# Program order for four engines in an expert loop, and a row finished in the front

## The chip, the cores and the metric

The kernel runs on one core of a Trainium2 chip. The metric is the device time of one execution in microseconds (us); lower is better. The engines are PE (TensorE, matrix products), DVE (VectorE), ACT (ScalarE), POOL (GpSimd) and SP (SyncE); each works off its own queue of instructions in order. Transfers run on 16 DMA engines, whichever engine issued them. Granted clock 1.00 means that TensorE runs at 2.4 GHz, 0.50 that it runs at 1.2 GHz.

## What is computed

One decoder layer on 512 tokens of width 1024, in float32. A mixer (a state-space branch and a block-sparse attention branch) is followed by a mixture of 32 experts, of which each token uses four. The part of the reference that matters here, cut:

```python
ada = cond @ ada_w[l] + ada_b[l]
sh_m, sc_m, gt_m, sh_f, sc_f, gt_f = split(ada, 6)
...
h2 = rms_norm(x, ffn_pre_g[l]) * (1.0 + sc_f) + sh_f
# moe_ffn(h2): every token goes to its top four experts
g = xb @ w_gate[e] + b_gate[e]
u = xb @ w_up[e] + b_up[e]
g = min(g, LIMIT); u = clip(u, -LIMIT, LIMIT)
yb = (g * sigmoid(ALPHA * g) * (u + 1.0)) @ w_down[e] + b_down[e]
y[row_tok] += yb * row_w
...
x = x + gt_f * rms_norm(ff, ffn_post_g[l])
```

The weights of one expert are three matrices of 1024 x 1024 floats (4 MB each), so the expert loop moves 384 MB of weights. `gt_f` is the last of the six gates that come from `ada_w`.

## The kernel before

**The front** (up to about 550 us) computes the mixer, the gates and the routing. `row_part` (lines 692 to 715) makes one half of one gate row: `cond_times` accumulates `ada_w` on DVE, a matmul with ones sums over the partitions. For the last gate (`name` is None) the row goes to `gfd` in memory as it is, a copy on ACT and a store on ACT's queue.

**The expert loop** (lines 1444 to 1458) walks over `jobs`. There are 32 slots, one expert each, sorted by how many tokens they hold; a slot has one or two blocks of 128, 64 or 32 tokens. A job is one of gate, up and down of a slot, in the order gate(n+1), down(n), up(n+1). `project` (line 1243) works a job off in four pieces of 1 MB of weights. Slots with a block of 128 split the weights into high halves (ACT, line 111) and low halves (DVE, line 112), one piece ahead of use, and multiply with three matmuls (lines 116 to 118). The other blocks multiply float32 weights as they are (line 1269).

**The weights** come through a ring of 11 chunks of 1 MB (`RINGS`), loaded by SP's queue (lines 1118 to 1122). A chunk is loaded again when the matmuls, or the splits, that read it are done.

**The small work of a slot.** `prep` (line 1164) makes a one-hot table `oh` on DVE and calls `tokens` (line 1194). `tokens` looks up the slot's rows with PE (line 1184), computes `src` and `dst` on DVE (lines 1205 and 1213) and issues the gather of the tokens into `xg` on POOL (line 1207). `weights` looks up the routing weights. `load` transposes `xg` on PE (line 1227 for blocks of up to 64, line 1237 for 128) through two PSUM buffers `tr`, and ACT or ACT and DVE copy the result out. Behind a job comes its stage function: `gate` (Silu on ACT), `up` (two DVE instructions into `s`, then the transposition of `s` into `a`), `down` (scaling on ACT into `yo`, then a scatter that adds into `yd`, issued by POOL at line 1313). `dst` has six buffers, `src` three, `oh` two.

**What sets the order.** `prep` and `weights` of slot n+1 are written ahead of the gate job of slot n, and `load` of slot n+1 is appended to `later` behind down(n-1). The rest goes through a list `later`: `follow(1)` behind each piece runs one entry of it. But these places only give priorities. A scheduler places each instruction on its engine, and may move it ahead of others or behind them by what it expects to be ready. POOL's order is set by hand only for a stretch before the loop (`manual_schedule` with POOL).

**The last row.** Behind the loop, `out_g` is loaded from `gfd` for all partitions, and two rows of 128 x 1024 (512 KB each, `ada_b` and `ffn_post_g`) are loaded by ACT's queue (line 1455) into `row`, which shares its buffers with the tokens of 128-token blocks, and are added to it and multiplied in on DVE (line 1456). The scheduler puts these into the loop where it finds room. The tail (from line 1473) normalizes the sum of the experts and writes the output.

Of the kernel before, what the change touches and what calls it, by code (L numbers as in the profile page):

```python
# [8 lines left out]
F32 = mybir.dt.float32  # L9
# [5 lines left out]
ALU = mybir.AluOpType  # L15
AX = mybir.AxisListType

P = 128
# [53 lines left out]
def tile_hybrid_block(ctx: ExitStack, tc: tile.TileContext, A, out):  # L72
# [611 lines left out]
    def bcast(src, off, n):  # L684
        return bass.AP(tensor=src.tensor, offset=src.offset + off, ap=[[0, P], [1, n]])
# [7 lines left out]
    def row_part(n, p):  # L693

        name, gain, c0 = (("gt_m", "mix_post_g", 2 * D), ("sh_f", None, 3 * D), ("sc_f", "ffn_pre_g", 4 * D),
                          (None, None, 5 * D))[n // 2]
        h = n % 2
        acc = p.tile([P, 512], F32, name="acc", bufs=2)
        cond_times(acc, c0 + 512 * h, 512)
        ps = ax_tile()  # L700
        if name is None:
            pe.matmul(ps[0:1], ones[:, 0:1], acc, start=True, stop=True)
            t = p.tile([P, 512], F32, name="acc", bufs=2)[0:1]
            act.activation(t, ps[0:1], AF.Copy)
            act.dma_start(gfd[:, 512 * h:512 * h + 512], t)
            return
        pe.matmul(ps, ones, acc, start=True, stop=True)
        b = p.tile([P, 512], F32, name="acc", bufs=2)
        act.dma_start(b, bcast(A["ada_b"], c0 + 512 * h, 512))
        r = rows[name][:, 512 * h:512 * h + 512]  # L710
        vec.tensor_add(r, ps, b)
        if gain:
            g = p.tile([P, 512], F32, name="acc", bufs=2)
            act.dma_start(g, bcast(A[gain], 512 * h, 512))
            vec.scalar_tensor_tensor(r, r, 1.0 if name == "sc_f" else 0.0, g, op0=ALU.add, op1=ALU.mult)
# [185 lines left out]
            wop.tile([P, 512], F32, name="m", bufs=2)  # L901
    for i in range(NT):
        act.dma_start(X1[i], xv[:, i])
    lg = keep.tile([P, NT, E], F32, name="lg")
    m8 = keep.tile([P, NT, 8], F32, name="m8")
    i8 = keep.tile([P, NT, 8], U32, name="i8")
# [236 lines left out]
    class Slot:  # L1143
# [15 lines left out]
            w = w[self.e:self.e + 1] if isinstance(self.e, int) else w[bass.ds(self.e, 1)]  # L1159
            return w.rearrange("o (k p) n -> p (o k) n", p=P)[:, 2 * q:2 * q + 2]  # L1160

        def prep(self):
            at_ = 0
            place = pos[:, :, self.rank:self.rank + 1] if self.e is None else pos_fix[:, :, self.e:self.e + 1]
            for m in self.blocks:
                oh = slp.tile([P, NT, P], BF16, name="oh", bufs=2)
                n = parts_of(m)
                shp = [P, NT, n, m]
                vec.tensor_tensor(oh[:, :, :n * m].rearrange("p i (n m) -> p i n m", n=n),
                                  iota_s[:, None, None, at_:at_ + m].to_broadcast(shp),  # L1170
                                  place[:, :, None, :].to_broadcast(shp), op=ALU.is_equal)
                oh = oh[:, :, :n * m]
                self.tokens(oh, m)
                at_ += m

        def weights(self):
            for oh, m in zip(self.oh, self.blocks):
# [16 lines left out]
        def tokens(self, oh, m):  # L1194
            p = self.lookup(oh, tab, m)
            r, n = rows_of(m), parts_of(m)
            self.oh.append(oh)
            tb = slp.tile([P, 3], F32, name="tb", bufs=2)[:r]
            vec.tensor_copy(tb, p)  # L1199
            tok = slp.tile([P, 1], F32, name="tok", bufs=2)[:r]  # L1200
# [42 lines left out]
        def project(self, stage):  # L1243
# [13 lines left out]
            for q in range(4):  # L1257
                ws = stream.get()
                for p, m, (xh, xl) in zip(ps, self.blocks, xs):
                    for k, (raw, wh, wl) in enumerate(ws):  # L1260
# [15 lines left out]
                        for n in range(2):  # L1276
                            c = slice(512 * n, 512 * n + 512)
                            mm3(p[:m, n], xh[:, kk], xl[:, kk], wh[:, c], wl[:, c], kk == 0, last)
                            if kk == 0:
                                pe.matmul(p[:m, n], pick[:, :m], bs[:, c], start=False, stop=False)  # L1280
                follow(1)
            later.append(lambda: getattr(self, stage)(ps))

        def shaped(self, p, t, m):

# [12 lines left out]
        def up(self, ps):  # L1298
            for p, m, s in zip(ps, self.blocks, self.s):
                u = sized("u", m)  # L1300
                pv, uu, uv = self.shaped(p, u, m)
                ss = self.shaped(p, s, m)[1]
                vec.tensor_scalar(uv, pv, LIMIT + 1.0, 1.0 - LIMIT, op0=ALU.min, op1=ALU.max)  # L1303
                vec.scalar_tensor_tensor(ss, ss, SILU_MAX, uu, op0=ALU.min, op1=ALU.mult)
            later.append(lambda: setattr(self, "a", [self.transposed(s, "a", m)
                                                     for s, m in zip(self.s, self.blocks)]))

        def down(self, ps):
            for p, m, w, idx in zip(ps, self.blocks, self.w, self.idx):
# [33 lines left out]
            self.used, w = self.ready.pop(0)  # L1343
            return w

    later = []

    def follow(n):
        for _ in range(min(n, len(later))):
            later.pop(0)()  # L1350

    kinds = {c: [] for c in "bwmhq"}
    kinds["q"] = [Slot(E - NFIX + e, BLOCKS[E - NFIX + e], e) for e in range(NFIX)]
# [10 lines left out]
    manual = tc.manual_schedule(engines={pool.engine})  # L1364
    manual.__enter__()
    for s in slots[:2]:
        s.prep()

    with tc.high_priority(PRIO):
# [71 lines left out]
    for s in slots[LOADS:2]:  # L1441
        s.load()
    nxt = 2
    for n, (s, stage) in enumerate(jobs):
        if stage == "gate" and n and nxt <= last:
            slots[nxt].prep()
            slots[nxt].weights()
        s.project(stage)
        if stage == "down" and nxt <= last:
            later.append(slots[nxt].load)  # L1450
            nxt += 1
    act.dma_start(out_g, bcast(gfd[:, :], 0, D))
    for src, off, op in ((A["ada_b"], 5 * D, ALU.add), (A["ffn_post_g"], 0, ALU.mult)):
        row = slp.tile([P, D], F32, name="row", tag="xg128")
        act.dma_start(row, bcast(src, off, D))
        vec.tensor_tensor(out_g, out_g, row, op=op)
    while later:
        follow(1)


    pc = tr_tile()
# [37 lines left out]
    with tc.For_i(0, n_more, 1):  # L1499
# [36 lines left out]
        stream = Stream(jobs)  # L1536
        for s, stage in jobs:
            s.project(stage)
            while later:
                follow(1)  # L1540
        vec.tensor_scalar(ctr, ctr, 1.0, None, op0=ALU.add)


# [39 lines left out]
```

## Time and profile before

| what | value |
|---|---|
| median of 3 runs | 1655.73 us (1652.3 to 1656.18) |
| profiled execution | 1651.96 us |
| its span | 1650.3 us |
| mean granted clock of TensorE | 0.937 |
| busy: PE, DVE, ACT, POOL | 1422.5, 673.3, 454.1, 244.8 us (86%, 41%, 28%, 15%) |
| moved by DMA | 507.98 MB, 308 GB/s over the span |
| loading a chunk of 1 MB, issue to landing | 15.2 to 15.8 us |
| expert loop by DMA traffic | about 560 to 1616 us |

The page gives sums over the whole span. The expert loop takes nearly two thirds of it, so the rows below are read from stretches of the loop: what each engine did in a window, how fast the DMA ran in it, and what an engine waited for. A timeline row gives the start and the length of a group of instructions, and in brackets how long the engine had been idle before it and what ended that. SyncE's "waits" are those of its issuing queue.

### The profile page before, as it was taken

To read this page: it belongs to the slowest core of one execution; us is meant where nothing else is said; L and a number is where in the kernel's file an instruction comes from. 1 tells how busy PE (TensorE), PEld (TensorE's weight loads), DVE (VectorE), ACT (ScalarE), POOL (GpSimd) and SP (SyncE) were. 2 spreads that over 40 slices of the span, in tenths; PEclk is the share of its full clock that TensorE was granted. 3 is DMA by queue.
4 is the path that set the end of the run, shared out by engine and by line. 5 is a ranking of instruction groups with operands and counts; after the bars stand their busy time and mean duration, and the time that the engine had idled before them with its cause. 6 is when DMAs were issued, how large, how long until landed. Compare 5 with 4: busy or idle time off the path is not lost. (4 is left out here: it accounts for less than half of the span.)

```text
span 1650.3 us, 24722 instructions
## 1 busy us (share of the span) xinstructions
PE 1422.5 (86%) x9498; PEld 756.3 (46%) x9498; DVE 673.3 (41%) x1487; ACT 454.1 (28%) x715; POOL 244.8 (15%) x244
## 2 busy tenths in 40 slices
PE   6899888799895899799969978997998998999871
PEld 2686776555574433234433335534534554433220
DVE  5896787687646200013421014313513355210003
ACT  5535333444542100002321023213402244101001
POOL 2200222200146101101111110011011011110101
PEclk9999999899997899999989998999999999999985
DMA  8433664253565999999999999999999789999995
GB/s 286 150 91 103 198 196 137 67 193 115 168 222 209 379 405 400 397 404 401 403 340 349 401 397 363 313 403 399 406 392 401 299 322 404 394 401 403 402 404 199
DMA packets 161000, 507.98 MB, mean 308 GB/s; under 512 B 19176, under 2 KB 21772, under 8 KB 160622
## 3 DMA queue, kind: packets, MB, share of 16 engines
q1 hardware_dynamic: 143000, 465.30, 73.5%
q0 software_dynamic: 11232, 26.74, 6.0%
q10 hardware_dynamic: 6646, 14.31, 2.7%
q8 instruction: 76, 1.25, 0.3%
q14 instruction: 46, 0.38, 0.1%
HBM read 482.97 MB, written 23.33 MB: 307 GB/s over the span
## 5 line engine op out<-in xcount | busy, mean ns | idle before, releaser
L1269 PE MATMUL acc<-raw,xt 128*32 128x256 f32 (+1 forms) x3712 | 475.4, 467 | 22.4 <-DMA raw<-in_w_up 15.2
L1269 PEld LDWEIGHTS acc<-raw,xt 128*32 128x32 f32 (+1 forms) x3712 | 148.5, 120 | 274.3 <-issue 192.8
L112 DVE TENSOR_TENSOR lo<-raw,hi 128x1024 fp32r<-128x1024 f32 x170 | 204.4, 1228 | 107.0 <-ACT hi L111 106.2
L1269 PE MATMUL acc<-raw,at 128*32 128x256 f32 (+1 forms) x1888 | 227.9, 459 | 10.7 <-DMA raw<-in_w_down 9.9
L1303 DVE TENSOR_SCALAR u<-acc 128x256 f32<-128x256 f32 (+2 forms) x44 | 26.7, 628 | 498.3 <-PE acc L1269 471.1
L111 ACT ACTIVATE hi<-raw 128x1024 fp32r<-128x1024 f32 x170 | 175.3, 1055 | 137.9 <-PE acc L118 59.2
L1313 POOL DMA_INDIRECT yd<-yo,dst x44 | 70.5, 1602 | 601.4 <-ACT yo L1312 467.3
L1269 PEld LDWEIGHTS acc<-raw,at 128*32 128x32 f32 (+1 forms) x1888 | 75.5, 119 | 141.0 <-issue 95.5
L1207 POOL DMA_INDIRECT xg<-h2d,src x44 | 50.2, 1140 | 372.0 <-DVE dst L1213 134.3
L1228 ACT ACTIVATE at<-tr 128x256 f32<-128x256 f32 (+1 forms) x39 | 18.0, 486 | 283.5 <-PE tr L1227 283.5
L116 PE MATMUL mm<-hTh,hi 128*128 128x512 f32 x192 | 78.8, 410 | 15.2 <-ACT stage L720 12.2
L1312 ACT ACTIVATE yo<-acc,w 128x256 f32<-128x256 f32 (+2 forms) x44 | 27.0, 638 | 231.4 <-PE acc L1269 189.3
L117 PE MATMUL acc<-lo,xh 128*128 128x512 f32 x160 | 67.8, 424 | 21.3 <-DVE lo L112 21.2
L116 PE MATMUL acc<-hi,xh 128*128 128x512 f32 x160 | 73.4, 459 | 8.5 <-ACT hi L111 8.5
L117 PE MATMUL mm<-hTl,hi 128*128 128x512 f32 x192 | 78.2, 408 | 0.0
L118 PE MATMUL mm<-hTh,lo 128*128 128x512 f32 x192 | 76.6, 403 | 0.0
L1295 ACT ACTIVATE s<-acc 128x256 f32<-128x256 f32 (+2 forms) x44 | 23.2, 547 | 162.6 <-PE acc L1269 133.0
L118 PE MATMUL acc<-hi,xl 128*128 128x512 f32 x160 | 66.0, 412 | 0.0
L1199 DVE COPY tb<-tr 128x3 f32<-128x3 f32 x44 | 6.7, 159 | 138.0 <-PE tr L1184 137.6
L248 DVE SCALAR_TENSOR_TENSOR acc<-raw,cond,acc 128x512 f32<-128x512 f32 x56 | 51.6, 921 | 0.2
L116 PEld LDWEIGHTS mm<-hTh,hi 128*128 128x128 f32 x192 | 37.1, 193 | 28.2 <-ACT stage L720 13.5
L117 PEld LDWEIGHTS acc<-lo,xh 128*128 128x128 f32 x160 | 32.1, 201 | 33.6 <-DVE lo L112 25.8
(580 smaller groups left out, 1972.6 us busy)
## 6 DMA issues: line engine op xcount, KB each, us to landing
raw<-in_w_up SPq DMA_DIRECT2D x97, 1024.0 KB, 15.8
raw<-in_w_gate SPq DMA_DIRECT2D x88, 1024.0 KB, 15.2
raw<-in_w_down SPq DMA_DIRECT2D x88, 1024.0 KB, 15.2
raw<-in_w_down SPq DMA_DIRECT2D x78, 512.0 KB, 15.6
raw<-in_w_gate SPq DMA_DIRECT2D x72, 512.0 KB, 15.4
raw<-in_w_up SPq DMA_DIRECT2D x60, 512.0 KB, 13.7
raw<-in_ada_w SPq DMA_DIRECT2D x48, 512.0 KB, 4.8
raw<-in_w_in SPq DMA_DIRECT2D x32, 512.0 KB, 4.6
```

Source lines behind the costliest of these rows:

```text
L111: act.activation(hv, src, AF.Copy)
L112: eng.tensor_sub(lv, src, hv)
L116: pe.matmul(o, sh, mh, start=start, stop=False)
L117: pe.matmul(o, sh, ml, start=False, stop=False)
L118: pe.matmul(o, sl, mh, start=False, stop=stop)
L248: vec.scalar_tensor_tensor(acc, w[:, k % 2], cond[:, k:k + 1], acc, op0=ALU.mult, op1=ALU.add)
L1207: pool.indirect_dma_start(out=xg[:r], out_offset=None, in_=h2d.rearrange("t (n c) -> (t n) c", n=n), in_offset=bass.IndirectOffsetOnAxis(a ...
L1269: pe.matmul(o, xh[:, kk], raw[:, c], start=(kk == 0), stop=last)
L1295: act.activation(sv, pv, AF.Silu, scale=ALPHA)
L1303: vec.tensor_scalar(uv, pv, LIMIT + 1.0, 1.0 - LIMIT, op0=ALU.min, op1=ALU.max)
L1312: act.activation(yv, pv, AF.Copy, scale=w)
L1313: pool.indirect_dma_start(out=yd.rearrange("t (n c) -> (t n) c", n=parts_of(m)), out_offset=bass.IndirectOffsetOnAxis(ap=idx[:, :1], axis= ...
```

## The change

1. The expert loop stands in a `manual_schedule` block for PE, DVE, ACT and POOL: on these four engines the instructions keep the order in which the program writes them. SP's queue is still placed by the scheduler.
2. `later` holds pairs of a due count and a function. `after(n, f)` makes `f` due n pieces later, and `follow()` behind each piece counts one on and runs all that is due. A stage function is due one piece after its job (in effect behind the first piece of the next job), the transposition of `s` two pieces after that, `prep` two and `weights` four pieces after the place where they stood, `load` three pieces after its down job.
3. `prep` is cut in two: `places` (the one-hot tables) keeps the place ahead of the gate job, `prep` calls `tokens` later.
4. The last gate's row is finished in the front: `row_part` adds the half of `ada_b` and multiplies with the half of `ffn_post_g` on one partition (1 x 512) before the store to `gfd`, and `out_g` is loaded in the front. The two loads of `row` and their two DVE operations behind the loop are gone.

```diff
@@ row_part
         if name is None:
             pe.matmul(ps[0:1], ones[:, 0:1], acc, start=True, stop=True)
-            t = p.tile([P, 512], F32, name="acc", bufs=2)[0:1]
-            act.activation(t, ps[0:1], AF.Copy)
-            act.dma_start(gfd[:, 512 * h:512 * h + 512], t)
+            t, g = (p.tile([P, 512], F32, name="acc", bufs=2)[0:1] for _ in range(2))
+            c = slice(512 * h, 512 * h + 512)
+            act.dma_start(t, A["ada_b"][:, c0 + 512 * h:c0 + 512 * h + 512])
+            vec.tensor_add(t, ps[0:1], t)
+            act.dma_start(g, A["ffn_post_g"][:, c])
+            vec.tensor_mul(t, t, g)
+            act.dma_start(gfd[:, c], t)
             return
@@ front, behind the loads of X1
+    act.dma_start(out_g, bcast(gfd[:, :], 0, D))
@@ Slot
-        def prep(self):
+        def places(self):
...
-                oh = oh[:, :, :n * m]
-                self.tokens(oh, m)
+                self.oh.append(oh[:, :, :n * m])
                 at_ += m
+
+        def prep(self):
+            for oh, m in zip(self.oh, self.blocks):
+                self.tokens(oh, m)
@@ project
-                follow(1)
-            later.append(lambda: getattr(self, stage)(ps))
+                follow()
+            after(1, lambda: getattr(self, stage)(ps))
@@ up
-            later.append(lambda: setattr(self, "a", [self.transposed(s, "a", m)
-                                                     for s, m in zip(self.s, self.blocks)]))
+            after(2, lambda: setattr(self, "a", [self.transposed(s, "a", m)
+                                                 for s, m in zip(self.s, self.blocks)]))
@@ the list
-    later = []
-
-    def follow(n):
-        for _ in range(min(n, len(later))):
-            later.pop(0)()
+    later, now = [], [0]
+
+    def after(n, f):
+
+        later.append((now[0] + n, f))
+
+    def follow(n=1):
+
+        now[0] += n or 0
+        while due := [x for x in later if n is None or x[0] <= now[0]]:
+            later.remove(due[0])
+            due[0][1]()
@@ the loop
-    for n, (s, stage) in enumerate(jobs):
-        if stage == "gate" and n and nxt <= last:
-            slots[nxt].prep()
-            slots[nxt].weights()
-        s.project(stage)
-        if stage == "down" and nxt <= last:
-            later.append(slots[nxt].load)
-            nxt += 1
-    act.dma_start(out_g, bcast(gfd[:, :], 0, D))
-    for src, off, op in ((A["ada_b"], 5 * D, ALU.add), (A["ffn_post_g"], 0, ALU.mult)):
-        row = slp.tile([P, D], F32, name="row", tag="xg128")
-        act.dma_start(row, bcast(src, off, D))
-        vec.tensor_tensor(out_g, out_g, row, op=op)
-    while later:
-        follow(1)
+    with tc.manual_schedule(engines={e.engine for e in (pe, vec, act, pool)}):
+        for n, (s, stage) in enumerate(jobs):
+            if stage == "gate" and n and nxt <= last:
+                slots[nxt].places()
+                after(2, slots[nxt].prep)
+                after(4, slots[nxt].weights)
+            s.project(stage)
+            if stage == "down" and nxt <= last:
+                after(3, slots[nxt].load)
+                nxt += 1
+        follow(None)
```

The order that results, at three places. In the listings a number behind a name only counts tiles; x4 at the end means four in a row.

PE, before, in the gate job of slot 10 (blocks of 64 and 32): its weights are `raw_6659` and `raw_6660` in the first piece, `raw2_6671` in the second; `xg64_6872` are the tokens of slot 11.

```order
L1274 MATMUL acc_6886<-b_gate_3804,perm3_3844 32x256
L1269 MATMUL acc_6886<-raw_6660,xt32_6831 32x256 x4
L1227 MATMUL tr_7058<-ident_74,xg64_6872 128x128 x4
L1269 MATMUL acc_6886<-raw2_6671,xt64_6824 64x512 x4
L1269 MATMUL acc_6886<-raw2_6671,xt32_6831 32x256 x8
```

PE, after, in the last two pieces of the up job of slot 10 and at the start of gate of slot 11, whose tokens are `xg64_6925`.

```order
L1276 MATMUL acc_7030<-raw_6872,xt64_6845 64x512 x2
L1276 MATMUL acc_7030<-raw_6873,xt64_6845 64x512 x2
L1276 MATMUL acc_7030<-raw_6872,xt32_6852 32x256 x4
L1276 MATMUL acc_7030<-raw_6873,xt32_6852 32x256 x4
L1234 MATMUL tr_7085<-ident_74,xg64_6925 128x128 x4
L1276 MATMUL acc_7030<-raw_6897,xt64_6845 64x512 x2
L1276 MATMUL acc_7030<-raw_6898,xt64_6845 64x512 x2
L1276 MATMUL acc_7030<-raw_6897,xt32_6852 32x256 x4
```

The transposition of slot 11's tokens moved from behind the first piece of gate(10) to behind the third piece of up(10).

DVE, before, ahead of the first piece of slot 14 (128 and 32 tokens): `tok`, `src` and `dst` belong to the two blocks of slot 16, the low halves `lo_7805` and `lo_7809` to slot 14.

```order
L1205 CAST src_8190<-tok_8187 128x1
L1213 SCALAR_TENSOR_TENSOR dst_8196<-tb_t_8194,padc64_3670,tok_8187 128x1
L1203 SCALAR_TENSOR_TENSOR tok_8207<-tok_8207,part32_3659 128x1
L1191 TENSOR_SCALAR tw__8219,w_8218<-tr_8220 128x3
L1205 CAST src_8210<-tok_8207 128x1
L1213 SCALAR_TENSOR_TENSOR dst_8216<-tb_t_8214,padc32_3664,tok_8207 128x1
L1191 TENSOR_SCALAR tw__8227,w_8226<-tr_8228 128x3
L1169 TENSOR_TENSOR oh_8478<-iota_s_3653,pos_4424 128x512
L112 TENSOR_TENSOR lo_7805<-raw2_7649,hi_7804 128x1024
L112 TENSOR_TENSOR lo_7809<-raw2_7649,hi_7808 128x1024
```

DVE, after, in gate of slot 14, from the second piece's low halves on; those of the first piece stand above these rows, `dst_7920` belongs to slot 15.

```order
L112 TENSOR_TENSOR lo_7838<-raw3_7654,hi_7837 128x1024
L112 TENSOR_TENSOR lo_7842<-raw3_7654,hi_7841 128x1024
L1310 TENSOR_SCALAR u32_7871<-acc_7747 128x256
L1311 SCALAR_TENSOR_TENSOR s32_7701<-s32_7701,u32_7871 128x256
L112 TENSOR_TENSOR lo_7877<-raw3_7681,hi_7876 128x1024
L112 TENSOR_TENSOR lo_7881<-raw3_7681,hi_7880 128x1024
L1206 COPY tb_7909<-tr_7904 128x3
L1208 SCALAR_TENSOR_TENSOR tok_7911<-tb_7909 128x1
L1210 SCALAR_TENSOR_TENSOR tok_7911<-tok_7911,part64_3676 128x1
L1212 CAST src_7914<-tok_7911 128x1
L1218 TENSOR_SCALAR tb_t_7918<-tb_7909 128x1
L1220 SCALAR_TENSOR_TENSOR dst_7920<-tb_t_7918,padc64_3679,tok_7911 128x1
```

The row numbers of a later slot stood ahead of the first low halves; now those of the next slot stand behind the low halves of three pieces.

ACT, before, in the last large slot (128 and 32 tokens): `row` is the tile that the two loads behind the loop fill, `hi` are high halves of the slot's weights.

```order
L1239 ACTIVATE xh_10580<-tr_10582 128x512
L1239 ACTIVATE xh_10580<-tr_10589 128x512
L1455 DMA row_12361<-in_ada_b 128x1024
L1295 ACTIVATE s64_10471<-acc_10362 128x512
L111 ACTIVATE hi_10421<-raw3_10171 128x1024
L111 ACTIVATE hi_10425<-raw3_10171 128x1024
L1455 DMA row_12364<-in_ffn_post_g 128x1024
L111 ACTIVATE hi_10437<-raw4_10181 128x1024
L111 ACTIVATE hi_10441<-raw4_10181 128x1024
```

ACT, after, at the same high halves.

```order
L1246 ACTIVATE ah_10401<-tr_10403 128x512
L1246 ACTIVATE ah_10401<-tr_10410 128x512
L1235 ACTIVATE at32_10417<-tr_10418 128x2x4x32
L111 ACTIVATE hi_10424<-raw3_10182 128x1024
L111 ACTIVATE hi_10428<-raw3_10182 128x1024
L111 ACTIVATE hi_10448<-raw4_10192 128x1024
L111 ACTIVATE hi_10452<-raw4_10192 128x1024
L1302 ACTIVATE s64_10482<-acc_10348 128x512
```

The two DMA issues are gone from between the high halves.

## Rows read from the trace of the kernel before

**Rows 1.** Windows view, loop in three parts; busy us (and instructions) by engine, clock, DMA

```profile
560.00:849.00 289.00, 266.70 (x2038) 109.66 (x2031) 61.58 (x159) 51.42 (x77) 32.63 (x24) 0.96 1.02 395
849.00:1420.00 571.00, 504.83 (x3832) 251.72 (x3830) 185.24 (x370) 148.47 (x194) 64.63 (x46) 0.95 0.98 374
1420.00:1616.00 196.00, 171.28 (x1248) 56.87 (x1247) 16.09 (x64) 14.82 (x29) 17.54 (x13) 0.95 1.03 398
```

**Rows 2.** Windows view, 40 us each; columns as in rows 1

```profile
680.00:720.00 40.00, 32.90 (x312) 12.49 (x308) 3.58 (x19) 2.91 (x6) 5.14 (x4) 0.83 1.03 400
720.00:760.00 40.00, 37.83 (x308) 13.05 (x298) 4.71 (x15) 4.72 (x9) 3.00 (x3) 1.00 1.03 406
...
840.00:880.00 40.00, 27.46 (x285) 12.50 (x284) 4.54 (x29) 3.65 (x6) 6.14 (x5) 0.83 0.82 288
...
1000.00:1040.00 40.00, 38.25 (x293) 23.28 (x292) 17.36 (x17) 13.24 (x15) 1.61 (x1) 0.97 0.93 349
1040.00:1080.00 40.00, 40.00 (x266) 18.92 (x266) 13.29 (x21) 12.95 (x17) 4.17 (x3) 1.00 0.93 328
...
1280.00:1320.00 40.00, 38.46 (x281) 21.11 (x280) 14.86 (x15) 11.38 (x14) 1.57 (x1) 1.00 0.76 298
1320.00:1360.00 40.00, 36.40 (x217) 20.69 (x216) 22.59 (x32) 19.56 (x23) 5.01 (x3) 0.96 0.89 320
```

**Rows 3.** Waits of PE in 849:1420; engine, line, waited for: total us, times, longest

```profile
PE acc L117 <- DVE lo L112: 23.5, 9, 11.2
PE tr L1227 <- DMA xg<-h2d,src: 12.5, 1, 12.5
PE acc L116 <- ACT hi L111: 12.4, 10, 1.7
PE tr L1227 <- DVE s L1304: 10.1, 10, 1.6
```

**Rows 4.** Timeline of PE around 865; start, us, engine, line, instruction, idle before

```profile
865.56 1.12 PE L1227 MATMUL tr<-ident,xg 128*128 128x128 f32 x4 [12.54 <-DMA xg<-h2d,src]
```

**Rows 5.** Timeline of POOL, 844 to 858; columns as in rows 4

```profile
844.93 1.61 POOL L1313 DMA_INDIRECT yd<-yo,dst  x1 [25.34 <-ACT yo L1312]
856.12 1.59 POOL L1313 DMA_INDIRECT yd<-yo,dst  x1 [9.58 <-DMA yd<-yo,dst]
858.02 1.02 POOL L1207 DMA_INDIRECT xg<-h2d,src  x1 [0.30 <-issue]
```

**Rows 6.** Timeline of DVE at three `dst` instructions; columns as in rows 4

```profile
985.80 0.22 DVE L1213 SCALAR_TENSOR_TENSOR dst<-tb_t,padc,tok 128x1 int32<-128x1 f32 x1 [2.90 <-DMA yd<-yo,dst]
...
994.01 0.22 DVE L1213 SCALAR_TENSOR_TENSOR dst<-tb_t,padc,tok 128x1 int32<-128x1 f32 x1 [7.73 <-DMA yd<-yo,dst]
...
1267.15 0.22 DVE L1213 SCALAR_TENSOR_TENSOR dst<-tb_t,pad_row,tok 128x1 int32<-128x1 f32 x1 [3.96 <-DMA yd<-yo,dst]
```

**Rows 7.** Timeline of PE around the start of slot 14; columns as in rows 4

```profile
958.54 0.98 PE L1237 MATMUL tr<-ident,xg 128*128 128x128 f32 x7 [0.53 <-ACT at L1228]
...
996.10 0.79 PE L117 MATMUL acc<-lo,xh 128*128 128x512 f32 x1 [11.24 <-DVE lo L112]
```

**Rows 8.** Windows view, behind stalls; columns as in rows 1

```profile
867.00:869.00 2.00, 2.00 (x6) 0.47 (x4) 0.00 (x0) 0.31 (x1) 0.00 (x0) 0.50 0.14 55
869.00:871.00 2.00, 2.00 (x30) 0.73 (x26) 0.04 (x1) 0.00 (x0) 0.00 (x0) 0.99 0.00 0
...
996.00:1002.00 6.00, 5.90 (x14) 4.03 (x15) 5.28 (x6) 1.06 (x1) 0.00 (x0) 0.50 1.03 410
```

**Rows 9.** Waits of SP's queue in 1290:1345; columns as in rows 3

```profile
SPq L1118 <- DVE src L1205: 20.5, 1, 20.5
```

**Rows 10.** Timeline of ACT at the first `row` load; columns as in rows 4

```profile
1320.84 0.33 ACTq L1455 DMA_DIRECT2D row<-in_ada_b  x1
```

**Rows 11.** Timeline of ACT in the front, the last gate row; columns as in rows 4

```profile
417.19 0.57 ACT L704 ACTIVATE acc<-ax 1x512 f32<-1x512 f32 x1
```

**Rows 12.** Timeline of DVE in the front, beside the second half; columns as in rows 4

```profile
438.42 0.69 DVE L848 SCALAR_TENSOR_TENSOR ga<-ga,mm 128x512 f32<-128x512 f32 x1 [4.72 <-DMA ga<-gd]
```

More of the change, by code (lines that the diff above doesn't have):

```diff
@@ L1171, in prep @@
                                   place[:, :, None, :].to_broadcast(shp), op=ALU.is_equal)
-                oh = oh[:, :, :n * m]
+                self.oh.append(oh[:, :, :n * m])
+                at_ += m
+        def prep(self):
+            for oh, m in zip(self.oh, self.blocks):
                 self.tokens(oh, m)
-                at_ += m
         def weights(self):
@@ L1196, in tokens @@
             r, n = rows_of(m), parts_of(m)
-            self.oh.append(oh)
             tb = slp.tile([P, 3], F32, name="tb", bufs=2)[:r]
@@ L1366, in tile_hybrid_block @@
     for s in slots[:2]:
+        s.places()
         s.prep()
@@ L1538, in tile_hybrid_block @@
             s.project(stage)
-            while later:
-                follow(1)
+            follow(None)
         vec.tensor_scalar(ctr, ctr, 1.0, None, op0=ALU.add)
```

## The prediction

> **What bounds the kernel now.** The page's 40 slices come first: the core's 16 DMA engines are near full from 560 us on, so the expert loop is a weight stream. The reader then asks of each stretch whether the stream ever stops. The loop in three parts [rows 1] gives 395 GB/s before the gate of slot 10, 374 in the middle, 398 behind slot 26. Only the middle part, 571 us long, is slower than the stream can be. In 40-us windows [rows 2] a full stretch runs at 400 to 406 GB/s (I use 403), and the loss is concentrated: 288 in 840–880, 349 and 328 in 1000–1080, 298 and 320 in 1280–1360. At 403 the missing bytes are 40 x (1 - 288/403) = 11.4 us, 5.4 + 7.4 = 12.8 us, and 10.4 + 8.2 = 18.6 us: 42.8 us together. This is the ceiling for anything that leaves the bytes of the loop alone.
>
> The DMA stops either because the ring of 11 chunks is full (TensorE is behind) or because the engine that issues the loads stands. Next, therefore, TensorE's own waits in the middle part [rows 3]: 23.5 us for DVE's low halves, 12.5 us in one piece for a gather, 12.4 us for ACT's high halves and 10.1 us for `s`. Each is then followed to its place.
>
> **Stall A, the gather.** In 853–865 TensorE does nothing; the transposes of slot 11's tokens wait 12.54 us for `xg` [rows 4]. GpSimd shows why the gather is late: the two scatters of slot 8 stand ahead of it, the second waits 9.58 us for the first to land, and the gather is issued only at 858.02 [rows 5]. The scheduler put these transposes right behind the first piece of gate(10).
>
> **Stall B, the row numbers.** At 985.80 and 994.01 DVE stands 2.90 and 7.73 us at `dst` [rows 6]: the buffer (six of them) still belongs to a scatter that has not landed. Behind it in DVE's order lie the low halves of slot 14's first piece, and TensorE waits 11.24 us for these [rows 7]. Two smaller waits of that kind cost TensorE 4.32 and 3.93 us, at 1135 and 1269; the DVE wait of the last one has its row [rows 6]. Sum 19.5 of the 23.5 us.
>
> **Half clock.** After each of the four stalls TensorE works at 1.2 GHz for a while: granted clock 0.50 in 996–1002 and 867–869, 0.99 in 869–871 [rows 8]. 6 us at half speed is 3 us lost; with 4 us at A and some 3 us at each of the two smaller ones it is about 8 us.
>
> **Stall C, the two rows.** SyncE stands 20.5 us in one piece in 1290–1345 [rows 9]. The profile names DVE's `src`, which had long been done; SyncE goes on when the `row` that ACT loads at 1320.84 [rows 10] has landed. No weights are issued meanwhile. The second `row` makes a shorter stand of the same kind.
>
> **The change, part by part, against the 1651.96 us of the profiled execution (span 1650.3).**
>
> *Program order on PE, DVE, ACT and POOL.* A: the transposes of slot n+2 now follow piece 3 of up(n+1), nine pieces behind the place where the gather is due. A 1 MB piece at 403 GB/s takes 2.6 us, so nine are 23 us. From the first scatter's start to the gather's landing it was 865.56 - 844.93 = 20.6 us, and the scatters start five pieces earlier still. The wait goes: -12.5. B: `tokens` of slot n+1 stand in gate(n), and the `dst` six back belongs to a slot scattered at least 12 pieces (31 us) earlier; a scatter lands in about 10 us. -19.5. The waits of the transposes for `s` go as well: TensorE now reaches these two pieces after the stage function is due, with some 5 us for two DVE instructions. I take -8 of 10.1. The half clock goes with the stalls: -8. The 12.4 us for the high halves stay, since a split is still made one piece ahead. TensorE's account of the middle part: 571 - 12.5 - 19.5 - 8 - 8 = 523 us.
>
> New waits, which the order of before mostly filled with other work: the transposition of a slot with a block of 128 and a smaller one needs three buffers of `tr` where two exist, so the third waits for ACT's and DVE's copies. In program order nothing else can be put between. The nearest row has 0.53 us for it, at 958.54, with other work in between [rows 7]; I take 0.8 for each of six (three such slots, x and a), 5 us. The bounds are 0 and 20 us (0.8 in each of some 25 transpositions of that part). The account becomes 528.
>
> *The row loads out of the loop.* DMA's account of the same part is 571 x 374/403 = 530 us. Two loads of 512 KB are 1 MB or 2.6 us of it, and SyncE no longer waits for them: 527. During C, TensorE was fed from the ring, so C by itself is worth between 0 and the 18.6 us of its windows; it is already inside the 527. The Trainium skill, page "DMA: Bandwidth & Descriptors", section "Issuing engines are not separate DMA queues", says that transfers from ScalarE, SyncE and GpSimd run on the same 16 engines, and that issuing from several only saves issue time. By it alone the two rows would cost their bytes, 2.6 us; the trace shows SyncE standing 20.5 us over the first alone, so the wait of an issuing queue is what counts here.
>
> *How the two accounts meet.* 528 and 527 are nearly the same, so a loss in one of them is not hidden by the other, piece by piece. In 1040–1080 TensorE is busy 40.00 of 40 us at clock 1.00 and the DMA still loses 7.4 us [rows 2]: the large slots take longer than their weights, and no wait can be removed there. I keep these 7 us. The middle part becomes 528 + 7 = 535, a gain of 36 us. The first and third parts run at 395 and 398 and keep their time: there the weights come last, and an order of engines doesn't change their bytes. The tail behind the last chunk keeps its order.
>
> *The front.* Two ACT copies of 0.57 us [rows 11] become four DVE operations on 1 x 512 elements and four small loads on ACT's queue. No row shows DVE at this shape from PSUM; the copy on ACT, 0.57, is nearest: 2.3 us of DVE work, near a place where DVE idles 4.72 us for `ga` [rows 12]. The `acc` tiles have two buffers, so the next accumulation waits until the first half's `gfd` store has been read out. Bounds -1 and +5 us; I take +2, as ACT's queue is in order and waits for those buffers ahead of gate work. The two DVE operations at the end (1.2 us each) were beside the stream: 0.
>
> Sum: 1652 - 36 + 2 = 1618. The runs shown are 0.3 to 4.2 us above the profiled one, so the forecast is 1620 us.
>
> **The rivals.** *(a) The new waits are common.* If in-order TensorE stands at each transposition, the extra 15 us (upper bound above) fall on a part in which it is the bound: 1652 - 36 + 15 + 2 + 2 = 1635. For it: TensorE's order had other matmuls there before. Against: with two pieces of distance their data is ready. *(b) Everything lost comes back.* 1652 - 42.8 - 2.6 + 2 = 1608; it needs the large slots to be covered by a ring that has more slack. *(c) The clock.* Without its lead TensorE waits for weights between pieces and drops to 1.2 GHz; 34 us of work at half speed takes 68 and gives all back: 1652, no change. For it: 680–720, where the stream is the bound, has clock 0.83. Against: the DMA runs at 400 GB/s there, so nothing was lost by it, and 720–760 has clock 1.00 [rows 2]. The Trainium skill, page "TensorE: Matmul & The Clock Gate", section "HAM oscillation — how this bites in real kernels", describes this: waits for DMA between tiles put TensorE back to half clock again and again. By it (c) would come out, 1652; the trace agrees only in the window at 0.83. *(d) Slower.* Program order puts the transposes of x into TensorE's stream for good. If a gather lands after they are due, all pieces behind them wait, as at A. The point from which it decides is nine pieces, 23 us, against GpSimd's wait for scatters (9.58 [rows 5]) and landing. If slots with two blocks pile up scatters so that three more stalls like A occur, 3 x 12.5 = 38 us take more than the gain: 1618 + 38 + 2 = 1658; five give 1683. Against: the scatters start 14 pieces, 36 us, before these transposes. That the order doesn't change is excluded by the order printed ahead.
>
> **How the numbers follow.** Forecast (1612 to 1628) 0.60; (a) and parts between 1628 and 1647, 0.19; (b) 0.10; (c) 0.05; (d) 0.06. A measurement of this kernel can tell about 0.3%, 5 us, from no change. Faster 0.89, same 0.05, slower 0.06. The range takes in (b) and (a) with the bounds of the front: 1604 to 1642.
>
> **What would show it.** In the trace of after: no TensorE wait over 5 us for `xg` or for the low halves between 840 and 1400; no DVE wait at `dst`; no SyncE stand near 1300; windows of 395 or more around 860 and 1300, with a dip left at the large slots 14 and 22. The middle part should be near 535 us, the front within 5 us of before. I am wrong if TensorE's waits at transposes add up to more than 15 us, if the clock in the middle part is below 0.95, or if the DMA stands at places where the ring is full for a reason not listed here.

## The result, and the profile after

The changed kernel takes 1614.14 us, median of four runs (1610.3 to 1617.6), against 1654.41 us before: a ratio of 0.9754 with an interval of 0.9731 to 0.9777, faster by 40 us. A second group of five runs on another occasion gave 1612.68 and a ratio of 0.9752 (0.9731 to 0.9773). The forecast was 1620. The profiled execution took 1610.3 us, its span is 1608.6 us, and its mean granted clock is 0.949.

The windows view, cut where the gates of slots 10 and 26 stand in this trace (columns as in rows 1):

```profile
560.00:847.00 287.00, 260.83 (x1994) 105.74 (x1988) 64.79 (x160) 51.06 (x76) 30.58 (x23) 0.98 1.02 394
847.00:1371.00 524.00, 489.00 (x3800) 241.92 (x3796) 186.04 (x350) 147.67 (x192) 66.22 (x45) 0.97 1.03 399
1371.00:1576.00 205.00, 177.58 (x1290) 59.45 (x1290) 21.18 (x81) 15.91 (x31) 18.60 (x14) 0.94 1.03 395
```

[rows 1] had 395, 374 and 398. The middle part is now as fast as the others: the stream of weights hardly stops, and 571 us became 524. The granted clock rose from 0.95 to 0.97 with it. The same view in 40-us windows:

```profile
800.00:840.00 40.00, 37.91 (x229) 20.86 (x227) 20.55 (x35) 12.38 (x15) 1.99 (x2) 1.00 0.96 373
840.00:880.00 40.00, 40.00 (x399) 15.56 (x400) 5.82 (x20) 5.00 (x9) 5.79 (x4) 1.00 0.99 364
...
1000.00:1040.00 40.00, 38.84 (x272) 21.41 (x272) 20.23 (x36) 13.47 (x17) 3.62 (x3) 1.00 1.03 405
1040.00:1080.00 40.00, 40.00 (x330) 14.59 (x330) 5.16 (x16) 3.41 (x7) 4.16 (x3) 1.00 1.04 389
...
1280.00:1320.00 40.00, 38.09 (x228) 19.87 (x224) 19.48 (x28) 18.28 (x22) 5.05 (x3) 1.00 1.03 396
1320.00:1360.00 40.00, 38.87 (x245) 25.04 (x244) 29.07 (x50) 20.55 (x25) 5.64 (x4) 1.00 1.03 400
...
1520.00:1560.00 40.00, 28.27 (x202) 9.01 (x203) 2.23 (x4) 2.05 (x4) 1.57 (x1) 0.85 1.03 403
```

These answer to [rows 2]. No window from 560 to 1560 is below 364, where 288, 349, 328, 298 and 320 had been. The largest loss that is left lies in 800 to 880 around slot 8, the largest slot: 40 x (1 - 373/403) + 40 x (1 - 364/403) = 6.9 us. TensorE is busy for 40.00 of 40 us in the second of these windows, as a bound engine is. The prediction had expected 395 GB/s or more around 860 and dips at the large slots 14 and 22; it came the other way round. The waits of TensorE in the middle part (columns as in rows 3):

```profile
PE acc L116 <- ACT hi L111: 13.1, 4, 3.5
PE acc L1276 <- DMA raw<-in_w_gate: 5.0, 6, 1.2
PE acc L1276 <- DMA raw<-in_w_down: 5.0, 4, 1.8
PE acc L117 <- DVE lo L112: 4.6, 9, 0.8
PE acc L1276 <- DMA raw<-in_w_up: 3.1, 4, 1.5
```

Of [rows 3], the 12.5 us for `xg` and the 10.1 us for `s` are gone, and 23.5 us for the low halves have become 4.6. New in the list of this part are the waits for weights, 13.1 us together: a sign that the stream is the bound. The waits for the high halves are fewer and longer, four with up to 3.5 us. ACT itself waits there for the weights, as its timeline shows at one of them:

```profile
1102.20 2.00 ACT L111 ACTIVATE hi<-raw 128x1024 fp32r<-128x1024 f32 x2 [3.21 <-DMA raw<-in_w_gate]
```

The answers to stalls A and B are short. The wait of TensorE for a gather that remains in the whole kernel is 1.8 us, at the first slot (view of the tile `xg`), and in the list of DVE's waits `dst` no longer waits for a scatter (before, 17.3 us in the middle part). [Rows 9] have no successor, as there is no `row`.

### The profile page after: what moved, and what is told of

It reads as the page before. It is cut to its first block, busy times and chain, and to the rows that moved or that the text cites. A ratio compares the mean times of both kernels' runs of the same rounds, so it can differ in the third digit from the quotient of the medians.

```text
span 1608.6 us, 24785 instructions
## 1 busy us (share of the span) xinstructions
PE 1408.9 (88%) x9498; PEld 746.6 (46%) x9498; DVE 685.4 (43%) x1489; ACT 454.3 (28%) x713; POOL 248.2 (15%) x244
## 5 line engine op out<-in xcount | busy, mean ns | idle before, releaser
L1276 PE MATMUL acc<-raw,xt 128*32 128x256 f32 (+1 forms) x3712 | 466.6, 463 | 42.8 <-DMA raw<-in_w_up 23.6
L1276 PEld LDWEIGHTS acc<-raw,xt 128*32 128x32 f32 (+1 forms) x3712 | 145.2, 119 | 293.8 <-issue 197.9
L1276 PE MATMUL acc<-raw,at 128*32 128x256 f32 (+1 forms) x1888 | 233.3, 464 | 21.7 <-DMA raw<-in_w_down 21.6
L1320 POOL DMA_INDIRECT yd<-yo,dst x44 | 73.9, 1680 | 561.9 <-ACT yo L1319 461.2
L116 PE MATMUL acc<-hi,xh 128*128 128x512 f32 x160 | 74.3, 464 | 13.1 <-ACT hi L111 13.1
L1235 ACT ACTIVATE xt<-tr 128x256 f32<-128x256 f32 (+1 forms) x39 | 18.0, 487 | 175.5 <-PE tr L1234 175.5
L116 PEld LDWEIGHTS mm<-hTh,hi 128*128 128x128 f32 x192 | 37.2, 194 | 28.2 <-ACT stage L724 13.6
L116 PEld LDWEIGHTS acc<-hi,xh 128*128 128x128 f32 x160 | 31.9, 199 | 28.9 <-ACT hi L111 18.7
L1247 DVE TENSOR_TENSOR xl<-tr,xh 128x512 fp32r<-128x512 f32 x10 | 6.4, 686 | 88.0 <-ACT xh L1246 88.0
```

The costliest lines, as they stand in the source:

```text
L116: pe.matmul(o, sh, mh, start=start, stop=False)
L1235: act.activation(h.rearrange("p (n j) t -> p j n t", n=n), pt.rearrange("p (j n t) -> p j n t", j=c, n=n), AF.Copy)
L1276: pe.matmul(o, xh[:, kk], raw[:, c], start=(kk == 0), stop=last)
L1320: pool.indirect_dma_start(out=yd.rearrange("t (n c) -> (t n) c", n=parts_of(m)), out_offset=bass.IndirectOffsetOnAxis(ap=idx[:, :1], axis= ...
```

## The experiments

The median of the kernel before was 1655.74 us beside the first four, 1656.86 beside the next four, and 1654.02 beside the last two. Since the start of the expert loop differs by several us between executions (below), I also give the **loop time**: from the first transposition of tokens on TensorE to the end of the span, read from the one profiled execution of each kernel. It is 1650.3 - 536.4 = 1113.9 us before and 1608.6 - 533.0 = 1075.6 us after, 38.3 us less. The two starts, and those of the runs below, are rows like these, the first of before, the second of after:

```profile
536.42 0.66 PE L1227 MATMUL tr<-ident,xg 128*128 128x128 f32 x2 [1.79 <-DMA xg<-h2d,src]
...
532.97 0.66 PE L1234 MATMUL tr<-ident,xg 128*128 128x128 f32 x2 [1.81 <-DMA xg<-h2d,src]
```

**The row alone.** The kernel before with the two edits that finish and load the last gate's row in the front.

```diff
+    act.dma_start(out_g, bcast(gfd[:, :], 0, D))
...
-    act.dma_start(out_g, bcast(gfd[:, :], 0, D))
-    for src, off, op in ((A["ada_b"], 5 * D, ALU.add), (A["ffn_post_g"], 0, ALU.mult)):
...
```

> Only the last gate's row is finished and loaded in the front; the loop keeps the scheduler's order. My theory: the stand of SyncE near 1303 was covered by a full ring while TensorE was the bound, so its removal gives at most the 2.6 us of the bytes, and the front gives between 0 and 3 us: 1648 to 1655. Rival, every byte that the stream loses is lost time: the 18.6 us of the windows 1280 to 1360 come back, about 1635.

Measured: 1646.25 us, ratio 0.9943 (0.9922 to 0.9964), 9 us faster; loop time 1648.4 - 541.9 = 1106.5, 7.4 less. That is more than the 2.6 us that I had allowed and far less than the rival's 18.6. Its windows tell why:

```profile
1280.00:1320.00 40.00, 38.46 (x293) 22.12 (x294) 16.14 (x15) 13.09 (x14) 1.57 (x1) 0.99 0.99 388
1320.00:1360.00 40.00, 37.10 (x219) 19.31 (x215) 18.97 (x27) 18.29 (x23) 5.09 (x3) 1.00 0.86 298
```

Before, 1280–1320 had 298 and 1320–1360 had 320 [rows 2], together 18.6 us lost. Without the rows the first has 388, but the second falls to 298: 1.5 + 10.4 = 11.9 us. So some two thirds of the loss at this place stay when SyncE has no rows to stand for; SyncE then waits for TensorE (34.9 and 13.5 us in 1280 to 1360). The size of slot 22, a large one, can't be the whole reason: the changed kernel has the same slot, and 396 and 400 here. The runs with twelve buffers, below, show more. I had put nearly all of stall C behind the ring; 7 us of it were on the path.

**The order alone.** The changed kernel with the row as it was.

> Program order and due counts as in the changed kernel, but the last row as before, with its two loads of 512 KB on ACT's queue behind the loop's code. My theory: stalls A and B are gone, and since the stream is now the bound, a stand of SyncE over these loads costs its full length less what is in flight: 10 to 20 us over the changed kernel, 1624 to 1634. Rival, the rows cost their bytes: 2.6 us, 1617.

Measured: 1623.64 us, ratio 0.98 (0.9775 to 0.9825), some 10 us above the changed kernel; loop time 1083.2, 7.6 above. SyncE stands 12.2 us for `row`, and one window of the stream falls (columns as in rows 3 and rows 1):

```profile
SPq L1118 <- DMA row<-in_ada_b: 12.2, 1, 12.2
...
1320.00:1360.00 40.00, 33.68 (x148) 21.11 (x145) 26.18 (x33) 19.00 (x21) 5.26 (x3) 0.96 0.94 344
```

40 x (1 - 344/403) = 5.9 us are lost there. The 10 us are the lower end of my 10 to 20, and the rival's 2.6 us for the bytes alone are out. By loop time the row is worth 7.4 us alone and 7.6 us in program order; with twelve buffers (below) it is 4.3 us, so it is not one figure for every loop.

**The due counts without program order.**

```diff
-    with tc.manual_schedule(engines={e.engine for e in (pe, vec, act, pool)}):
+    if True:
```

> The changed kernel without the block that keeps program order: due counts, the split of prep and the row in the front stay, the scheduler orders the loop. My theory: the scheduler again moves the row numbers and the transposes of x ahead, so both stalls stay and the time is that of the row change alone, 1640 to 1655. Rival, the due counts do the work by the places where the code is written: 1612 to 1620.

Measured: 1646.36 us, ratio 0.9932 (0.9908 to 0.9956): the median of the row alone, as I expected. The loop time, 1644.7 - 530.4 = 1114.3, is 7.8 us longer than there and that of the kernel before; the loop of this profile only began earlier. So the due counts without the order give nothing, and may cost some us. Both stalls are back (waits of TensorE, 780 to 1400):

```profile
PE acc L117 <- DVE lo L112: 16.5, 8, 8.8
PE tr L1234 <- DMA xg<-h2d,src: 14.0, 2, 12.5
```

The places in the code are only hints to the scheduler; it moved `dst` (16.3 us of waits for scatters on DVE in this stretch) and the transpositions ahead again. The block that keeps the order carries the gain. On which of the four engines the order is needed was not run.

**Stall B alone.** The kernel before, with

```diff
-            dst = slp.tile([P, 1], I32, name="dst", bufs=6)[:r]
+            dst = slp.tile([P, 1], I32, name="dst", bufs=12)[:r]
```

and the same order of instructions on every engine.

> The kernel before with twelve buffers of dst in place of six; nothing else moves. My theory: the three DVE waits at dst go, and with them 19.5 us of TensorE's waits and some 5 us at half clock, of which the stream can give back 13 to 25 us: 1630 to 1641. Rival, the stream was running during the stall (402 GB/s in 985 to 996), so nothing is won: 1650 to 1656.

Measured: 1632.92 us, ratio 0.9871 (0.9838 to 0.9903), 23 us faster; loop time 1090.8, 23.1 less. One number of buffers is more than half of the change. TensorE's longest wait for low halves falls from 11.2 to 2.1 us, and the windows at slot 14 recover:

```profile
840.00:880.00 40.00, 27.78 (x224) 12.47 (x223) 3.84 (x29) 2.78 (x4) 6.13 (x5) 0.83 0.82 286
1000.00:1040.00 40.00, 38.25 (x285) 20.97 (x284) 16.15 (x16) 14.40 (x18) 1.61 (x1) 1.00 1.03 406
1040.00:1080.00 40.00, 40.00 (x294) 18.37 (x294) 9.64 (x18) 9.71 (x14) 4.17 (x3) 1.00 1.03 389
```

[Rows 2] had 349 and 328 for the second and third. So the 7.4 us in 1040–1080, where TensorE was busy for the whole window, went with stall B too. My reading is that the stall had filled the ring, so that the stream stopped 40 us later, while TensorE worked off the backlog at full speed. The run shows only that the dip goes with the stall; the trace of before agrees, with the stream at 402 GB/s in a window in which TensorE did nothing:

```profile
985.00:996.00 11.00, 0.00 (x0) 0.00 (x0) 2.47 (x11) 1.03 (x2) 3.59 (x3) 0.51 1.04 402
```

The first of the three windows still has 286: stall A is where it was.

**B and C together.** Twelve buffers and the row in the front, in the scheduler's order.

> The kernel before with twelve buffers of dst and the row in the front: stalls B and C are taken away, in the scheduler's order, only A and the short waits at transposes are left. If the three stalls add up: the 1633 of twelve buffers less the 9 of the row, 1622 to 1627, and the changed kernel's last 8 to 12 us are A's. Rival, once the stream is the bound either edit covers the other: 1630 to 1634.

Measured: 1622.67 us, ratio 0.9796 (0.9756 to 0.9835); loop time 1086.5. The edits add up by the medians: 23 and 9 would give 1624. By loop time they don't quite: 23.1 and 7.4 would give 1083.4, and the row is worth 1090.8 - 1086.5 = 4.3 us here. The 8.5 us to the changed kernel (10.9 in loop time) I put down to A and the short waits; that is by difference, since no run takes A alone away. This run still has their rows:

```profile
PE tr L1232 <- DMA xg<-h2d,src: 12.1, 1, 12.1
...
PE tr L1232 <- DVE s L1309: 10.1, 10, 1.6
```

The place of stall C in five runs, in the order before, the row alone, twelve buffers alone, both, and the changed kernel:

```profile
1240.00:1440.00 200.00, 180.12 (x1355) 99.25 (x1355) 82.91 (x141) 66.94 (x82) 24.16 (x16) 0.96 0.95 363
1240.00:1440.00 200.00, 179.57 (x1360) 99.88 (x1360) 83.05 (x143) 67.22 (x83) 22.63 (x15) 0.96 0.98 371
1240.00:1440.00 200.00, 182.56 (x1340) 99.96 (x1334) 83.07 (x140) 66.94 (x82) 23.45 (x16) 0.96 1.00 384
1240.00:1440.00 200.00, 184.69 (x1372) 99.58 (x1360) 81.62 (x141) 67.31 (x83) 27.04 (x16) 0.97 1.02 391
1240.00:1440.00 200.00, 191.17 (x1385) 99.20 (x1385) 82.92 (x142) 64.14 (x80) 24.72 (x16) 0.97 1.03 399
```

Against 403 these are 20, 16, 9, 6 and 2 us. Twelve buffers alone, with the rows still in the loop, take more away here than the rows do: more than half of what I had called stall C goes with the six buffers. The nearest wait of that kind is the one at 1267 [rows 6]; that it alone is behind it isn't shown.

**Stall A made again, in program order.** The changed kernel with the transposition of x due seven pieces earlier.

```diff
+                after(4, slots[nxt].load)
...
-                after(3, slots[nxt].load)
```

> The changed kernel, with the transposes of the next slot's tokens due four pieces after the gate job starts, two pieces behind the gather's issue, in place of eleven. My theory, the distance is what removes stall A: a gather takes about 8 us from src to landing, two pieces give 3 to 5 us, so in-order TensorE stands 3 to 4 us in most slots; 16 slots of the middle part use up its slack there (490 us busy in 525) and more: 1640 to 1665, slower than or near the kernel before. Rival, the distance doesn't matter as long as the order is kept: 1612 to 1620.

Measured: 1630.29 us, ratio 0.9848 (0.9804 to 0.9892): 16 us slower than the changed kernel, and still 27 faster than before. The waits are those I expected (waits of TensorE, 560 to 1600):

```profile
PE tr L1234 <- DMA xg<-h2d,src: 52.2, 27, 4.0
PE tr L1244 <- DMA xg<-h2d,src: 23.9, 5, 6.0
```

76 us of waits, 28.2 + 20.2 of them in 780 to 1390, but only 20 us of loop time (1096.0). The 19 waits of 780 to 1390 come to the lower end of the 48 to 64 us that 16 waits of 3 to 4 us would be, but in the whole loop a wait is 2.4 us on average. Their price is what I got wrong: where the stream is the bound, a wait of TensorE falls into time in which it would wait for weights. Its waits for weights in 560 to 1600 fall from 62.5 us in the changed kernel to 17.1. The price is paid at the large slots:

```profile
800.00:880.00 80.00, 71.68 (x541) 35.64 (x539) 26.32 (x49) 18.13 (x25) 7.79 (x6) 0.94 0.88 325
1040.00:1080.00 40.00, 38.23 (x272) 18.23 (x273) 10.93 (x18) 9.16 (x13) 4.21 (x3) 0.97 0.90 324
1320.00:1360.00 40.00, 38.35 (x214) 21.49 (x212) 20.11 (x26) 17.32 (x19) 5.89 (x3) 1.00 0.95 339
```

Against 403 these lose 15.5 + 7.8 + 6.4 = 29.7 us, and the same windows of the changed kernel 8.5. The distance of the transposition behind its gather matters, which is what the rival denied.

**Program order with the old list.** Row in the front and program order, with `prep` and `weights` whole ahead of the gate job and one entry of the list behind each piece.

> The kernel before with the row in the front and program order on the four engines, but with the old list: prep and weights whole ahead of the gate job, one entry of the list behind each piece. My theory: the order alone isn't enough; TensorE stands 2 to 4 us at the lookups of each gate job, which wait for the one-hot table and the copies of DVE, and about 1 us more at the transposes one piece after the stage function: 50 to 80 us in the middle part, of which the slack takes up to 35: 1625 to 1665. Rival, the due counts add nothing to the order: 1612 to 1620.

Measured: 1620.71 us, ratio 0.9793 (0.9753 to 0.9833); the interval overlaps that of the changed kernel, and the loop time is 1082.9, 7.3 us above it. My 1625 to 1665 is missed; the order is nearly everything, the due counts some us. The lookups do wait (waits of TensorE, 560 to 1600), but again they cost a fraction of their length:

```profile
PE tr L1189 <- DVE oh L1174: 35.5, 16, 6.8
```

**A slot order for the rest.** Slots 5 and 7 exchanged, so that slot 8 has slots of 32 tokens on both sides.

```diff
-ORDER = "qqmhmqmhbqmhmqbhmqwhmqbhwqmhmhhq"
+ORDER = "qqmhmhmqbqmhmqbhmqwhmqbhwqmhmhhq"
```

> The changed kernel, with the slots at places 5 and 7 exchanged, so that the largest slot (8, blocks of 128 and 64) has 32-token slots on both sides. The stream of the changed kernel loses about 7 us in 800 to 880, where the ring is full behind slot 8. My theory: four down pieces of 1.0 in place of 1.9 us give 3 to 4 us of it back, 1608 to 1613. Rival, the loss stays since it is slot 8's own work: 1612 to 1618.

> The changed kernel once more, beside the next one on the same chip, for a direct comparison: 1610 to 1618. It also gives a second profile of it, to see by how much the start of the expert loop differs between executions of one kernel: by the profiles so far 530 to 542 us in kernels with one and the same front, so several us.

> The exchange of slots 5 and 7 once more, beside the changed kernel. My theory: 3 us less than the changed kernel, which is the loop's difference in the two profiles (1072.5 against 1075.6 us): 1607 to 1614, ratio to it 0.998. Rival: no difference.

Measured: 1611.11 us (1608.89 to 1615.9) the first time; beside the changed kernel, 1609.3 (1607.41 to 1613.22) against 1612.68 (1609.09 to 1617.19), which is a ratio of 0.998. The ranges overlap, so the runs' times alone don't prove it. The loop times are 1072.5 and 1072.2 against 1075.6 and 1076.2, and the windows of the pair show where 3 to 4 us come from, the changed kernel first:

```profile
760.00:920.00 160.00, 157.26 (x1105) 69.57 (x1105) 51.48 (x106) 40.04 (x53) 19.22 (x14) 1.00 1.01 387
920.00:1080.00 160.00, 149.30 (x1235) 70.78 (x1232) 50.03 (x101) 38.77 (x52) 19.25 (x14) 0.97 1.03 399
...
760.00:920.00 160.00, 155.56 (x1182) 70.81 (x1176) 52.35 (x107) 40.72 (x55) 21.53 (x15) 1.00 1.03 396
920.00:1080.00 160.00, 148.17 (x1226) 69.92 (x1226) 49.40 (x97) 38.87 (x52) 18.85 (x13) 0.97 1.03 399
```

160 x (396 - 387)/403 = 3.6 us less is lost around slot 8, and nothing differs later. It is the fastest version of this study, by little, and that it is faster rests on the loop times and windows, not on the medians.

## Why the prediction was right, step by step

**Stall A** went, as argued: nine pieces are enough, and two are not (the early load). Its worth was put at 12.5 us and some half clock. The runs show 8.5 to 11 us for it and the short waits at transpositions together, by difference. Where it had stood, the changed kernel still loses the 6.9 us around slot 8.

**Stall B** went; its 19.5 us and the half clock behind them were sized well (23 us by twelve buffers). The step that failed here is "no wait can be removed there" on the window 1040–1080. I read a window with a busy TensorE as a loss of its own and kept 7 us for it. The twelve buffers removed it: it went with B, as its echo by the reading above. What I should have asked of that window is why the ring was full when it began.

**Stall C**: two parts are mis-sized, both ways. In the sum I gave the rows 2.6 us of bytes; by loop time they were worth 7.4 and 7.6 us, alone and in program order, and 4.3 with twelve buffers. The Trainium skill ("DMA: Bandwidth & Descriptors", "Issuing engines are not separate DMA queues") says that transfers run on the same 16 DMA engines, whichever engine issued them. An estimate from that alone is the 2.6 us of the bytes; all three measurements are above it, with SyncE's queue standing until the rows had landed. Of the windows' 18.6 us, which I named as the upper bound, 11.9 stayed without the rows. The prediction put this place down to SyncE's stand alone; the larger part went with the buffers of `dst`.

**The new waits**: six of about 1 us in the whole loop (5.8 us), behind DVE's copies, against six of 0.8 in the sum. Here is one, on TensorE's timeline:

```profile
963.19 1.09 PE L1244 MATMUL tr<-ident,xg 128*128 128x128 f32 x8
965.26 0.44 PE L1234 MATMUL tr<-ident,xg 128*128 128x128 f32 x2 [0.98 <-DVE xl L1247]
```

Rival (a), that they are common, did not come.

**The meeting of the two accounts.** Middle part: 535 forecast, 524 measured. Third part: no change forecast; between the first bias matmul of gate 26 and the end it took 1608.6 - 1372.0 = 236.6 us against 1650.3 - 1421.0 = 229.3 us, 7.3 more. My reading is one cause for both. Before, the stalls had left the ring full when TensorE came to slot 26; now the stream is the bound, and TensorE arrives there with less in store. The windows agree: from 560 us to that gate the stream moved 289 x 0.395 + 571 x 0.374 = 327.7 MB before [rows 1] and 287 x 0.394 + 524 x 0.399 = 322.2 MB after. Of the 5.5 MB less, 1 MB is the two rows, and some 1.4 MB (3.4 us at 0.4 MB per us) came ahead of 560, since this execution's loop began earlier. Three MB are left, three chunks or 8 us. Cutting at TensorE's gates moved these 7 us from one part to the other. From the start of the loop to that matmul it is 1421.0 - 536.4 = 884.6 us before and 1372.0 - 533.0 = 839.0 after, 45.6 less; with the 7.3 more behind it 38.3 us are left, in place of 36. So near a hit is in part luck: the 7 us that I had kept for the window came back, but 6.9 us are lost around slot 8, where SyncE waits for TensorE (36.3 us of waits in 800 to 880) and where I had expected a full stream. Rival (b) had put the ceiling at 1608; what is missing to it is of the size of these 6.9 us.

**The front**: +2 forecast. The four DVE operations are there, each 0.67 to 0.68 us where I took 0.57 from ACT's copy, so 2.7 us of DVE work:

```profile
416.38 0.68 DVE L706 TENSOR_TENSOR acc<-ax,acc 1x512 f32<-1x512 f32 x1
419.31 0.67 DVE L708 TENSOR_TENSOR acc<-acc 1x512 f32<-1x512 f32 x1
438.53 0.68 DVE L706 TENSOR_TENSOR acc<-ax,acc 1x512 f32<-1x512 f32 x1
442.79 0.67 DVE L708 TENSOR_TENSOR acc<-acc 1x512 f32<-1x512 f32 x1
```

What they do to the start of the loop can't be read. The first transposition of tokens starts at 530.4 to 541.9 us in nine profiles with the new front and at 536.4 to 540.4 in three with the old one (533.0 and 531.2 for two executions of the changed kernel). The 3.4 us by which it was earlier in the profile shown first is inside that. The means are 534.6 and 538.8, the other way round than forecast, but the scatter is larger than the difference: the term stays open, with its sign. The sum of the prediction was 1618 for the profiled execution, which took 1610.3: of the 7.7 us, 2.3 are the loop's and 5.4 the start's.

**The clock rival (c)** fell. TensorE waits for weights in most slots now (62.5 us in 78 waits from 560 to 1600; before, 32.2 us in 39 from 560 to 1620), yet the granted clock of the middle part rose to 0.97. It is 0.85 in 1520–1560, where the last small slots leave TensorE idle for 12 of 40 us, and the stream runs at 403 GB/s there. The Trainium skill ("TensorE: Matmul & The Clock Gate", "HAM oscillation — how this bites in real kernels") describes the drop itself, which that window agrees with; a loss of time that goes with it isn't seen there, with the stream at its full rate.

**Rival (d)** did not come in the changed kernel, where TensorE waits for one gather, 1.8 us, at the first slot. In the run that sets the transpositions two pieces behind the gather its mechanism is real, and its price is wrong: there are 32 stalls, and the kernel is still 27 us faster than before.

## What to carry to other kernels

Where engines wait in order behind one late instruction, look for the place of that instruction in the queue before its duration: twelve buffers in place of six moved 23 us without one instruction less, and an order kept as written 32 (the order-only run). When a stream is behind a ring, a low window of the stream can be the echo of a stall 40 us earlier; undo the stall alone before calling the window a bound. And once the stream is the bound, a wait of TensorE costs a fraction of its length: 76 us of waits cost 20, paid at the large slots, so keep distances long enough there and leave the rest.

## What was not expected of the hardware

Transfers issued by one engine held another engine's queue: SyncE stood 20.5 us before [rows 9], and 12.2 us in the order-only run, until the rows of ACT's queue had landed, though it does not read them. The semaphores that the traces record with each instruction (counters that a transfer raises when it lands) show that this comes from the program. The loop's loads on SyncE's queue take eight semaphores in turn, and each of the two rows takes one of the same eight. A load that comes next on such a semaphore waits for the row, and so do all loads behind it. In the kernel before this is semaphore 103: the row's last increment is at 1324.12 us, and SyncE's wait for it ends at 1324.13.

Most of that stand is not the transfer. SyncE had issued its last load by 1303.6, and ACT came to the issue of the row only at 1320.84 [rows 10]: 17 us of the 20.5 lie ahead of the issue, 3.3 between issue and landing. In the order-only run it is 5.7 us of the 12.2. A single late issue on another queue is enough to stop a stream that shares its semaphores; giving the rows semaphores of their own was not run.
